# A two-layer diffusion trunk on one core: tap order, transposes on row halves, low parts of weights by accumulating transfers, and another layer-norm pacing

## The chip, the core and the metric

The kernel runs on one core of a Trainium2 chip. The metric is the device time of one execution in microseconds (us). The engines named below are PE (TensorE, matmuls; its weight loads are listed as PEld), DVE (VectorE), ACT (ScalarE), POOL (GpSimd) and SP (SyncE, which here only starts transfers).

## The reference

A trunk of two layers works on 256 latent tokens and 256 context tokens of width 1024. Each layer, cut to what matters here (the first six numbers of `mod`/`mod_c` are shifts, scales and gates made from the conditioning vectors):

```python
h  = modulate(rmsnorm(x,  norm1_g[l]), sh1, sc1)
hc = modulate(rmsnorm(xc, norm1_g[l]), csh1, csc1)
p  = h @ w_in[l]                       # GLU pair | q k v | branch gates
q, k = rope_2d(q), rope_2d(k)          # latent rows only
y_conv = conv_branch(p[..., :GLU_END], conv_dw[l], conv_dw_b[l], conv_ln_g[l], conv_ln_b[l], w_conv_out[l])
y_attn = merge_heads(neighbourhood_attention(q, k, v, k_c, v_c, na_rpb[l])) @ w_na_out[l]
x  = x + g1 * gated_merge(p[..., QKV_END:], y_conv, y_attn, w_out[l])
h2 = modulate(rmsnorm(x, norm2_g[l]), sh2, sc2)
x  = x + g2 * conv_ffn(h2, w_up[l], ffn_dw[l], ffn_dw_b[l], w_down[l])

def conv_branch(p_glu, dw, dw_b, ln_g, ln_b, w_o):
    a, g = jnp.split(p_glu, 2, axis=-1)
    u = dwconv1d(a * jax.nn.sigmoid(g), dw, dw_b)      # 31 taps, 512 channels
    return jax.nn.silu(layernorm(u, ln_g, ln_b)) @ w_o
```

Attention has 8 heads of 64; a latent query sees a window of the latent grid with a learned bias and all context keys under one softmax. In layer 0 the context tokens pass through the same weights and attend to each other; in layer 1 they give keys and values only. The output is the latent stream after a last RMS norm.

## The kernel before

Tokens stand in columns, channels in partitions. In layer 0 a matmul has 512 moving columns (256 latent and 256 context tokens), in layer 1 mostly 256.

**Weights.** They come in units of 128x1024 (512 KB). SP loads a unit into one of four buffers `raw` (L147 and L157 start loads), ACT rounds it to a high part `whi` (L160), DVE subtracts to get the low part `wlo` (L161); both have four buffers as well. `wunit` does this for one unit. Each product is three passes, `mm3` (L179 to L181): high weight by high activation, high weight by low activation, low weight by high activation. A group is one accumulation over a unit's eight blocks, 24 matmuls; in the two output branches of the token mixer it is twelve, and a unit has two groups. After a group, and in layer 0 also in its middle, `slot()` lets the side work run a step: taps, attention, the layer norm, modulation.

**Attention.** Class `Attention` takes head pairs as their queries and keys become ready. `products` computes scores of two heads on the 64-row halves of PE (L440). `scores` adds the bias and takes the maximum on DVE (L458), ACT exponentiates and sums, DVE inverts, ACT scales. `turn` transposes the probabilities, 128x128 at a time (L494 for latent queries, L499 for context), 16 transposes a turn, into the PSUM banks `sc`, `sc`, `pt` and `main`; ACT copies each bank to `pT`. `values` multiplies with V (L512) on 64-column tiles. `step` decides by a count of slots when the next turn, values and products are issued; in one step the turn of the scores before comes first, then the values of the turn before, then new products. There are six turns in layer 0 and four in layer 1.

**Convolution.** Each of four channel blocks has 31 taps on DVE (`conv_tap`, L591), issued two or three a slot; in layer 0 two `u` buffers hold the GLU outputs, so that taps of block j must be out before block j + 2 is written. The layer norm follows as side work: the four blocks are summed (two adds on POOL, L842 and L843, one on DVE), a matmul with ones (L847) gives the sum over channels, then squares, `rstd`, and the scaling.

**Modulation.** Part of the modulation numbers for later is made by `ada_dots`: DVE multiplies a 128x1024 weight tile with a broadcast row and sums (L271, two dots a tile), and part by `ada_half`, 32-column matmuls (L202) with transposes behind them (L228). The tiles come through the same four `raw` buffers. The number `pace[0]` says how many dot steps a slot makes.

**Behind attention** of layer 0 stand the remaining gates, the neighbourhood output branch (`U_NA`, with a gate multiply on DVE behind each group, L885) and the convolution output branch (`U_CO`, L890 to L893).

**Order.** The program is built once: the framework fixes the order of the instructions on each engine when it is built, by its own estimate of when each can run. `issue_after` adds an ordering to this. Each engine then executes its list in order and waits at the head of it.

Of the kernel before, what the change touches and what calls it, by code (L numbers as in the profile page):

```python
# [8 lines left out]
F32 = mybir.dt.float32  # L9
# [28 lines left out]
U_GLU0, U_V, U_IN, U_NA, U_CO, U_WO, U_UP, U_DN = 0, 2, 6, 36, 40, 44, 52, 96  # L38
NU = 118
T_GLU, T_Q, T_K, T_GATE = 0, 6, 10, 14  # L40

# [4 lines left out]
def trunk(ctx: ExitStack, tc: tile.TileContext, xt, cvec, crow, wall, wada, params, bias_t, rope_t, out):  # L46
# [136 lines left out]
    def group(ps, ws, xh, xl, c):  # L183
# [201 lines left out]
    class Attention:  # L385

        def __init__(self, l, eb, T, V, oh, ol):
            self.l, self.eb, self.T, self.V, self.oh, self.ol = l, eb, T, V, oh, ol  # L390
            self.todo, self.soft, self.pv, self.n, self.at = [], [], [], 0, 0
            self.ctx, self.pairs, self.last = [], 0, None

# [22 lines left out]
        def step(self, now=False):  # L416
            self.n += 1
            since = self.n - self.at
            if not now and (since < (4 if self.todo else 3 if self.soft else 2) or not self.todo and self.pairs < 4):
                return  # L420
            if self.todo and not now and self.n - self.todo[0][0] < 2:
                return
            self.at = self.n
            pv, self.pv = self.pv, []
            soft, self.soft = self.soft, []
            for what, its, pps in soft:
                with tc.issue_after(self.last.ins), tc.issue_after(self.done.ins):
# [3 lines left out]
            if self.todo:  # L431
                _, what, its = self.todo.pop(0)
                outs = [self.products(it, [psum(t) for t in tags]) for it, tags in zip(its, (("sc", "sc"), ("pt", "main")))]
                self.soft.append((what, its, [(self.scores if what == LAT else self.ctx_scores)(it, o) for it, o in zip(its, outs)]))

# [15 lines left out]
        def scores(self, it, out):  # L451
            qt, bt = it[1], it[-1]
            pps = []
            for i, ps in enumerate(out):

                mx = small([P, 1], "mx")
                p2, b2 = ps.rearrange("p (a k) -> p a k", a=2), bt[:, 2 * qt + i :: 4 - 2 * qt - i, :]
                dve.tensor_tensor_reduce(p2, p2, b2, -1.0, 3.0e38, ALU.add, ALU.min, mx)  # L458
                pp = self.eb.tile([P, 512], F32, tag="pp", bufs=4, name=nm("pp"))
                sm = small([P, 1], "sm")  # L460
                self.exp = act.activation(pp, ps, AF.Exp, bias=mx, scale=-1.0, accum_out=sm)
                ri = small([P, 1], "ri")
                dve.reciprocal(ri, sm)
                self.done = act.mul(pp, pp, ri)
                pps.append(pp)
            return pps

        def ctx_scores(self, it, out):
            pps = []
            for ps in out:  # L470
                mx = small([P, 2], "mx2")
                dve.tensor_reduce(mx, ps.rearrange("p (q k) -> p q k", q=2), AX.X, ALU.max, negate=True)
                pp = self.eb.tile([P, 512], F32, tag="pp", bufs=4, name=nm("pp"))
# [12 lines left out]
        def turn(self, what, its, pps):  # L486

            pts = [self.eb.tile([P, 4, S], F32, tag="pT", bufs=4, name=nm("pT")) for _ in range(2)]
            for n, tags in enumerate((("sc", "sc"), ("pt", "main"))):
                for i, pp in enumerate(pps[n]):  # L490
                    pt = psum(tags[i])
                    if what == LAT:
                        for kt in range(4):
                            pe.transpose(sl(pt, kt), sl(pp, kt), ident)  # L494
                        act.copy(pts[i][:, :, n * P : (n + 1) * P], pt.rearrange("p (k q) -> p k q", k=4))
                    else:
                        for t in range(2):
                            for kt in range(2):
                                pe.transpose(pt[:, kt * S + t * P : kt * S + (t + 1) * P], sl(pp, 2 * t + kt), ident)  # L499
                        act.copy(pts[i][:, 2 * n : 2 * n + 2, :], pt.rearrange("p (k q) -> p k q", k=2))  # L500
            js = [its[0][0]] if what == LAT else [it[0] for it in its]
            self.pv.append((what, js, pts))

        def values(self, what, js, pts, bank):
            po = psum(bank)
            kts = range(4) if what == LAT else range(2, 4)
            for n, j in enumerate(js):
                c = slice(n * S, (n + 1) * S)
                for kt in kts:
                    for i in range(2):  # L510
                        h = 2 * j + i
                        pe.matmul(  # L512
                            po[i * HD : (i + 1) * HD, c], self.V[kt][:, h * HD : (h + 1) * HD],
                            pts[i][:, 2 * n + kt - kts[0], :], start=kt == kts[0], stop=kt == kts[-1],
                        )
# [42 lines left out]
    for l in range(DEPTH):  # L558
# [5 lines left out]
        with ExitStack() if last else start as e1a:  # L564
# [17 lines left out]

            taps = []

            def conv_tap(j, t):
                w = par[:, l * NPAR + DW + j * TAPS + t : l * NPAR + DW + j * TAPS + t + 1]
                src = us[j % NU_][:, :, t : t + S]
# [4 lines left out]

            rate = [0]

            def conv_run():
                while True:
                    for _ in range(rate[0]):
                        if taps:
# [34 lines left out]
            with ExitStack() as e1b:  # L633
                eb = e1b.enter_context(tc.tile_pool(name=f"eb{l}", bufs=1))
                V = [eb.tile([P, CONV], F32, name=f"V{l}_{t}") for t in range(4)]
                att = Attention(l, eb, T, V, oh, ol)

# [107 lines left out]
                conv = conv_run()  # L745
                rate[0] = 3 if last else 2
                add_side(conv)
# [68 lines left out]
            with ExitStack() as e1c:  # L816
# [15 lines left out]
                def layer_norm():  # L832

                    while taps:
# [14 lines left out]
                    for j in range(KC):  # L849
                        dve.scalar_tensor_tensor(flat[j], pm[:, :T], -1.0 / CONV, flat[j], ALU.mult, ALU.add)  # L850
                        s2.add(flat[j], j == KC - 1)
                    yield
                    yield
                    pb = yield from rstd(s2, CONV, "po")
                    for j in range(KC):
# [7 lines left out]
                        yield  # L863
                    pace[0] = 0.4

# [359 lines left out]
```

## Time and profile before

| | us |
|---|---|
| three runs, median (lowest to highest) | 1127.05 (1126.9 to 1127.49) |
| the profiled execution | 1127.64 |
| its span, first to last instruction | 1125.9 |
| PE busy in it | 1114.1 |
| PE weight loads | 963.0 |
| DVE busy | 908.3 |
| ACT busy | 563.6 |
| POOL busy | 14.7 |

The mean granted TensorE clock is 0.998 of full speed. A row of a group reads: line, engine, operation, output and inputs, shape, count, then busy time in us and mean ns of one, then the idle time ahead of them and what ended it. A row of a timeline begins with its start and its length in us from the span's start. A matmul's length contains its way through the array; how fast they follow each other is read from start to start. Layer 0's attention lies between about 80 and 200 us, the stage behind it to 330 us.

### The profile page before, as it was taken

Reading aid. Unit: us, or ns where it says so; the run is one execution under the profiler, and the core shown is the slowest. Engines: PE = TensorE matmul, PEld = TensorE weight load, DVE = VectorE, ACT = ScalarE, POOL = GpSimd, SP = SyncE. Lnnn points to the kernel's source line nnn. Section 1 sums busy time; section 2 is a strip of 40 time slices with the busy share of each in tenths; the row PEclk is TensorE's granted clock in tenths of the full one; section 3 lists DMA queues with packets and bytes.
Section 4 is the critical chain, followed back from the end, with each engine's and each line's share of the span. In section 5 each row is a group of like instructions: output and inputs, shape, how many; then the busy total and the mean of one; then the engine's idle time right before and its main releaser. Section 6 shows DMA issues by size and latency. Waiting matters only on the chain.

```text
span 1125.9 us, 17731 instructions
## 1 busy us (share of the span) xinstructions
PE 1114.1 (99%) x6828; PEld 963.0 (86%) x6828; DVE 908.3 (81%) x1631; ACT 563.6 (50%) x934; POOL 14.7 (1%) x24
## 2 busy tenths in 40 slices
PE   9999999999999999999999999999999999999997
PEld 7778777787789988888888888989888999999997
DVE  5689999685778788888898555789996898988773
ACT  4347657542333543434343222544677667766642
POOL 0000000000000000000000000000000000000000
PEclk9999999999999999999999999999999999999999
DMA  9833231536734354554556665556433575565781
GB/s 364 282 94 103 75 118 38 206 97 214 245 118 138 114 161 150 168 169 149 168 171 215 219 191 186 180 181 187 145 126 121 167 250 163 188 194 181 219 268 58
DMA packets 53941, 190.83 MB, mean 169 GB/s; under 512 B 6240, under 2 KB 6496, under 8 KB 53856
## 3 DMA queue, kind: packets, MB, share of 16 engines
q1 hardware_dynamic: 53568, 189.65, 52.1%
q8 instruction: 54, 0.88, 0.3%
q14 instruction: 31, 0.25, 0.1%
q10 hardware_dynamic: 288, 0.04, 0.0%
HBM read 188.62 MB, written 1.05 MB: 168 GB/s over the span
## 4 chain that ended last, share of the span: by engine, by line
PE 83%; DVE 9%; issue 6%; ACT 2%; DMA 0%; POOL 0%; POOLq 0%; DVEq 0%; SPq 0%; ACTq 0%
PE main L179 24%; PE main L181 24%; PE main L180 24%; DVE cb L591 4%; PE main L644 4%; DVE wlo L161 1%; PE sc L181 1%; PE sc L179 1%; PE sc L180 1%; PE po L202 1%; PE po L512 1%; PE sc L129 1%; PE sc L440 0%; DMA sb<-in_crow 0%; PE sc L494 0%
## 5 line engine op out<-in xcount | busy, mean ns | idle before, releaser
L179 PE MATMUL main<-h,whi 128*128 128x256 f32 (+1 forms) x1328 | 446.7, 337 | 0.0
L181 PE MATMUL main<-h,wlo 128*128 128x256 f32 (+1 forms) x1328 | 442.9, 335 | 1.0 <-DVE wlo L161 1.0
L180 PE MATMUL main<-h,whi 128*128 128x256 f32 (+1 forms) x1328 | 442.2, 334 | 0.1
L160 ACT CAST whi<-raw 128x1024 fp32r<-128x1024 f32 (+1 forms) x244 | 252.3, 1039 | 285.5 <-PE main L180 131.5
L161 DVE TENSOR_TENSOR wlo<-raw,whi 128x1024 fp32r<-128x1024 f32 (+1 forms) x244 | 292.9, 1207 | 112.5 <-ACT whi L160 108.0
L179 PEld LDWEIGHTS main<-h,whi 128*128 128x128 f32 x1328 | 249.4, 188 | 32.1 <-issue 3.6
L181 PEld LDWEIGHTS main<-h,wlo 128*128 128x128 f32 x1328 | 249.3, 188 | 29.6 <-DVE wlo L161 1.5
L180 PEld LDWEIGHTS main<-h,whi 128*128 128x128 f32 x1328 | 249.8, 188 | 28.5 <-DVE h L367 0.5
L591 DVE SCALAR_TENSOR_TENSOR cb<-u,par,cb 128x512 f32<-128x512 f32 (+1 forms) x240 | 140.4, 609 | 1.4
L271 DVE CUSTOM_DVE_ANT_0 t<-raw,sb,par 128x1024 bf16<-128x1024 f32 x100 | 126.7, 1277 | 1.0 <-ACT sb L255 0.7
L179 PE MATMUL main<-fh,whi 128*128 128x256 f32 (+1 forms) x386 | 123.0, 319 | 0.0
L180 PE MATMUL main<-fl,whi 128*128 128x256 f32 (+1 forms) x386 | 122.9, 319 | 0.0
L181 PE MATMUL main<-fh,wlo 128*128 128x256 f32 (+1 forms) x386 | 122.9, 318 | 0.0
L180 PEld LDWEIGHTS main<-fl,whi 128*128 128x128 f32 x386 | 72.7, 188 | 5.6
L179 PEld LDWEIGHTS main<-fh,whi 128*128 128x128 f32 x386 | 72.7, 188 | 5.6
L181 PEld LDWEIGHTS main<-fh,wlo 128*128 128x128 f32 x386 | 72.7, 188 | 5.5
L963 ACT ACTIVATE t<-main,par 128x512 f32<-128x512 f32 (+1 forms) x82 | 50.6, 667 | 39.0 <-PE main L181 39.0
L964 DVE SCALAR_TENSOR_TENSOR t<-main,par,t 128x510 f32<-128x510 f32 (+1 forms) x82 | 47.5, 615 | 10.2 <-ACT t L963 9.8
L967 DVE SCALAR_TENSOR_TENSOR t<-main,par,t 128x510 f32<-128x510 f32 (+1 forms) x82 | 46.6, 609 | 0.0
L366 ACT ACTIVATE h<-t,mod 128x256 fp32r<-128x256 f32 x56 | 25.4, 502 | 36.1 <-DVE t L365 36.1
L898 DVE SCALAR_TENSOR_TENSOR x<-main,mod,x 128x256 f32<-128x256 f32 x48 | 22.1, 479 | 23.5 <-PE main L181 23.3
L644 PE MATMUL main<-whi,h 128*128 128x512 f32 x128 | 40.6, 402 | 0.1
(221 smaller groups left out, 1188.2 us busy)
## 6 DMA issues: line engine op xcount, KB each, us to landing
raw<-in_wall SPq DMA_DIRECT2D x239, 512.0 KB, 4.2
raw<-in_wada SPq DMA_DIRECT2D x88, 512.0 KB, 4.3
bias<-in_bias_t SPq DMA_DIRECT2D x8, 640.0 KB, 4.8
row<-in_wada SPq DMA_DIRECT2D x8, 512.0 KB, 4.7
sb<-in_crow SPq DMA_DIRECT2D x5, 512.0 KB, 6.0
x<-in_xt SPq DMA_DIRECT2D x8, 256.0 KB, 4.4
raw<-in_wall SPq DMA_DIRECT2D x8, 256.0 KB, 7.1
out<-t SPq DMA_DIRECT2D x3, 256.0 KB, 2.1
```

The costliest lines, as they stand in the source:

```text
L160: act.copy(hi[:, c], r[:, c])
L161: dve.tensor_tensor(lo[:, c], r[:, c], hi[:, c].bitcast(F32), ALU.subtract)
L179: pe.matmul(ps, w[0], xh, start=start, stop=False)
L180: pe.matmul(ps, w[0], xl, start=False, stop=False)
L181: pe.matmul(ps, w[1], xh, start=False, stop=stop)
L271: dve.tensor_tensor_reduce(tmp().bitcast(BF16), r, v, 1.0, pr(l, BADA + n, 1), ALU.mult, ALU.add, mods[l][:, n, s : s + 1])
L366: high = act.activation(hi[:, c], y[:, c], AF.Identity, bias=b)
L591: dve.scalar_tensor_tensor(cb[j], src, w, cb[j], ALU.mult, ALU.add)
L644: mm = pe.matmul(pv[t], h1[n == 1][k][:, c], w[n == 2][:, b], start=k + n == 0, stop=k == KD - 1 and n == 2)
L963: act.activation(c, pv_, AF.Identity, bias=pr(l, FDB + t, 1), scale=w[1])
L964: dve.scalar_tensor_tensor(c[:, :, 1:], pv_[:, :, : S - 1], w[0], c[:, :, 1:], ALU.mult, ALU.add)
L967: dve.scalar_tensor_tensor(c[:, :, : S - 1], pv_[:, :, 1:], w[2], c[:, :, : S - 1], ALU.mult, ALU.add)
```

## The change

1. **Turning on row halves.** `turn` issues each 128x128 transpose as two, for rows 0 to 63 and 64 to 127, with 64 columns of the identity moving, into two banks; a turn is 32 transposes. `pT` is one tile for two heads, the copies write it in another layout.
2. **Low parts by transfers.** For 26 units (`ADDED`: 19 in layer 0, 7 in layer 1, all among GLU, query, key and gate units) the new `wadded` lets ACT write the high part and its negative, and POOL starts an accumulating transfer that adds `raw`. The memory for POOL's transfer descriptors is set to 1024.
3. **Taps.** Each tap is ordered behind the score maximum issued last. Layer 0 has four `u` buffers instead of two, and three taps a slot instead of two. In `step`, layer 0 can issue a turn without new products; the products then come in the next step (`late`).
4. **Layer norm of layer 0.** All three block sums are on DVE; four slots pass instead of two before `rstd`; `pace[0]` is 0.2 during the norm and 1.0 behind it (1.0 and 0.4 before). Layer 1 keeps its values.

```diff
+ADDED = {*((0, U_IN + i) for i in range(19)), *((1, U_IN + i) for i in (7, 8, 9, 14, 15, 16, 17))}
...
+    def wadded(l, u):
+
+        r = raw_unit(wall[l, u])
+        hi = wp.tile([P, UW], F32R, tag="whi", bufs=4, name=nm("whi"))
+        lo = wp.tile([P, UW], F32R, tag="wlo", bufs=4, name=nm("wlo"))
+        act.copy(hi, r)
+        act.mul(lo, hi.bitcast(F32), -1.0)
+        pool.dma_start(lo, r, accum_op=ALU.add)
+        return hi, lo
+
     def unit8(l, u, at=None):
-        w = wunit(l, u, at)
+        w = wadded(l, u) if (l, u) in ADDED else wunit(l, u, at)
...
-            if not now and (since < (4 if self.todo else 3 if self.soft else 2) or not self.todo and self.pairs < 4):
+            alone = not self.l and self.soft and not self.pv and not self.late
+            if not now and since < (4 if self.todo or alone else 3 if self.soft else 2) and not self.late:
                 return
-            if self.todo and not now and self.n - self.todo[0][0] < 2:
+            if not now and not alone and not self.todo and self.pairs < 4:
                 return
+            if not now and not alone and self.todo and self.n - self.todo[0][0] < 2:
+                return
+            if self.late:
+                self.late, self.at = False, self.n
+                return self.issue()
+            if alone and not now:
+                self.late = True
...
-                dve.tensor_tensor_reduce(p2, p2, b2, -1.0, 3.0e38, ALU.add, ALU.min, mx)
+                self.after[0] = dve.tensor_tensor_reduce(p2, p2, b2, -1.0, 3.0e38, ALU.add, ALU.min, mx)
...
+                outs = [psum(t).rearrange("p (i s q) -> p i s q", i=2, s=4) for t in tags]
                 for i, pp in enumerate(pps[n]):
...
+                    for s in range(4):
+                        src = s if what == LAT else s % 2 * 2 + s // 2
+                        for pt, r in zip(outs, HALF):
+                            pe.transpose(pt[:, i, s], sl(pp, src)[r], ident[r, r])
+                for pt, r in zip(outs, HALF):
...
-                        for kt in range(4):
-                            pe.transpose(sl(pt, kt), sl(pp, kt), ident)
...
-            NU_ = KC if last else 2
+            NU_ = KC
...
             def conv_tap(j, t):
+                if after[0] is not None:
+                    with tc.issue_after(after[0].ins):
+                        tap(j, t)
+                else:
+                    tap(j, t)
...
-                rate[0] = 3 if last else 2
+                rate[0] = 3 if last else 3.0
...
-                    pace[0] = 1.0
+                    pace[0] = 1.0 if last else 0.2
...
-                    pool.tensor_tensor(sm[:, :T], flat[0], flat[1], ALU.add)
-                    pool.tensor_tensor(sm[:, :T], sm[:, :T], flat[2], ALU.add)
+                    eng = pool if last else dve
+                    eng.tensor_tensor(sm[:, :T], flat[0], flat[1], ALU.add)
+                    eng.tensor_tensor(sm[:, :T], sm[:, :T], flat[2], ALU.add)
...
-                    yield
-                    yield
+                    for _ in range(2 if last else 4):
+                        yield
...
-                    pace[0] = 0.4
+                    pace[0] = 0.4 if last else 1.0
...
-    nc = bacc.Bacc("TRN2", target_bir_lowering=False, num_devices=1)
+    nc = bacc.Bacc("TRN2", target_bir_lowering=False, num_devices=1, dynamic_dma_scratch_size=1024)
```

Lines of the changed kernel in the rows below: L180 to L182 are the three passes, L162 the low part on DVE, L199 and L200 ACT's two passes of an added unit, L213 the 32-column matmuls, L282 the dots, L463 the products, L518 the transposes, L921 the gate multiply.

PE, layer 0, around the first turn, before: a unit group, the turn, the products of the next pair.

```order
L181 MATMUL main_972<-h_189,wlo_975 128x512
L494 MATMUL sc_1009<-ident,pp_845 128x128 x4
L494 MATMUL sc_1015<-ident,pp_853 128x128 x4
L494 MATMUL pt_1021<-ident,pp_861 128x128 x4
L494 MATMUL main_1027<-ident,pp_869 128x128 x4
L440 MATMUL sc_1033<-qk_967,qk_921 128x512
L440 MATMUL sc_1034<-qk_967,qk_921 128x512
```

The same place of the change; rows that repeat a pair are left out.

```order
L182 MATMUL main_945<-h_189,wlo_949 128x512
L518 MATMUL sc_984<-ident,pp_861 128x64
L518 MATMUL sc_985<-ident,pp_861 128x64
...
L518 MATMUL pt_1004<-ident,pp_877 128x64
L518 MATMUL main_1005<-ident,pp_877 128x64
...
L180 MATMUL main_1035<-h_182,whi_1038 128x512
```

The transposes come in pairs into two banks, and the unit group's next matmuls, not the products, follow this turn.

DVE, layer 0, around the second unit of the neighbourhood branch, before (`g` a gate, `t_` and `mod` a dot and its sum):

```order
L885 TENSOR_TENSOR g_9_2284<-main_2603,g_9_2284 128x512
L161 TENSOR_TENSOR wlo_2679<-raw_2677,whi_2678 128x1024
L885 TENSOR_TENSOR g_10_2332<-main_2628,g_10_2332 128x512
L271 ISA t_2703,mod_108<-raw_2701,sb_2022,par 128x1024
L271 ISA mod_108 128x1
L271 ISA t_2705,mod_108<-raw_2701,sb_2025,par 128x1024
```

The low part 2679 stands here ahead of the second unit's gate multiplies and is used by the third unit. In the change the same place reads:

```order
L921 TENSOR_TENSOR g_9_2405<-main_2710,g_9_2405 128x512
L162 TENSOR_TENSOR wlo_2737<-raw_2735,whi_2736 128x1024
L282 ISA t_2756,mod_108<-raw_2754,sb_2160,par 128x1024
L282 ISA mod_108 128x1
L282 ISA t_2758,mod_108<-raw_2754,sb_2163,par 128x1024
```

The low part behind the multiply of `main_2710` is now that of the second unit itself. On PE the change reads there:

```order
L182 MATMUL main_2710<-oh_3_205,wlo_2671 128x512
L180 MATMUL main_2741<-oh_0_202,whi_2736 128x512
L181 MATMUL main_2741<-ol_0_206,whi_2736 128x512
L180 MATMUL main_2761<-oh_0_202,whi_2736 128x512
L181 MATMUL main_2761<-ol_0_206,whi_2736 128x512
L213 MATMUL sc_2768<-raw_2769,sil 32x256 x4
L182 MATMUL main_2741<-oh_0_202,wlo_2737 128x512
```

Both groups of the unit begin with their high parts, half a visit to the 32-column tiles stands between, and then comes the first matmul that needs the low part 2737. Before, the twelve matmuls of a group stood together and the visit in one piece.

More of the change, by code (lines that the diff above doesn't have):

```diff
@@ L385, in trunk, with __init__ @@
     class Attention:
-        def __init__(self, l, eb, T, V, oh, ol):
+        def __init__(self, l, eb, T, V, oh, ol, after):
+            self.after = after
             self.l, self.eb, self.T, self.V, self.oh, self.ol = l, eb, T, V, oh, ol
             self.todo, self.soft, self.pv, self.n, self.at = [], [], [], 0, 0
-            self.ctx, self.pairs, self.last = [], 0, None
+            self.ctx, self.pairs, self.last, self.late = [], 0, None, False
         def pair(self, j, q, k, bt, last):
@@ L430, in step, with issue @@
                 self.values(*work, "sc" if work[0] == CTX and not (soft or self.todo) else "po")
[L431 to L434, printed above, removed]
+            if self.todo and not self.late:
+                self.issue()
+        def issue(self):
+            _, what, its = self.todo.pop(0)
+            outs = [self.products(it, [psum(t) for t in tags]) for it, tags in zip(its, (("sc", "sc"), ("pt", "main")))]
+            self.soft.append((what, its, [(self.scores if what == LAT else self.ctx_scores)(it, o) for it, o in zip(its, outs)]))
         def product(self, out, q, k, c, d):
```

30 lines of the change are left out of this document (16 added, 14 removed).

## The prediction

> **What bounds the kernel now.** I read the page first, then the windows of the attention stretch and of the stage behind it, then the timeline at one turning, and last the groups kept apart by shape.
>
> ```profile
> span 1125.9 us, 17731 instructions
> PE 1114.1 (99%) x6828; PEld 963.0 (86%) x6828; DVE 908.3 (81%) x1631; ACT 563.6 (50%) x934; POOL 14.7 (1%) x24
> L181 PE MATMUL main<-h,wlo 128*128 128x256 f32 (+1 forms) x1328 | 442.9, 335 | 1.0 <-DVE wlo L161 1.0
> 100.00:120.00 20.00, 20.00 (x131) 16.15 (x130) 20.00 (x39) 16.72 (x34) 0.00 (x0) 1.00 0.44 138
> 160.00:180.00 20.00, 20.00 (x124) 15.61 (x124) 20.00 (x39) 15.56 (x29) 0.00 (x0) 1.00 0.28 79
> 260.00:280.00 20.00, 20.00 (x111) 14.95 (x110) 10.40 (x17) 4.61 (x7) 0.00 (x0) 1.00 0.59 194
> ```
>
> The page's first part gives PE 1114.1 of 1125.9 us, at a granted clock of 1.00 in these windows. A window reads: its bounds, its length, then the busy time of PE, PEld, DVE, ACT and POOL with their counts, the clock, the DMA share and GB/s. In the two windows of layer 0's attention DVE is as full as PE, 20.00 of 20. Yet the low-part matmuls of the whole program (L181) wait 1.0 us in sum for DVE's low parts. So DVE is full there with work that has no early deadline, the taps, and PE sets the pace. Taking load from DVE moves nothing by itself; the time changes only where PE's own instructions get shorter or more numerous, or where a new wait reaches PE. Behind attention DVE is half empty (10.40 of 20 in the last row).
>
> The profiled execution took 1127.64 us, its span and 1.7 us around it; the median of the three runs is 0.6 lower. I sum against 1127.64 and take off 0.6 at the end.
>
> **Turning on row halves.** Before, a turn is 16 transposes of 128 rows; ten turns make 160. Now each transpose is a pair, rows 0 to 63 and 64 to 127, each with 64 moving columns, into two banks.
>
> ```profile
> 100.45 0.39 PE L181 MATMUL main<-h,wlo 128*128 128x512 f32 x1
> 100.68 1.04 PE L494 MATMUL sc<-ident,pp 128*128 128x128 f32 x8
> 101.55 0.60 PE L494 MATMUL pt<-ident,pp 128*128 128x128 f32 x4
> 101.99 0.60 PE L494 MATMUL main<-ident,pp 128*128 128x128 f32 x4
> 102.52 1.16 PE L440 MATMUL sc<-qk,qk 64*128 64x512 f32 x6
> ```
>
> Eight transposes from 100.68 to 101.55 are 0.109 us each; 160 of them 17.4 us. A 512-column matmul takes the 0.23 us from 100.45 to 100.68, 0.45 ns a column, a transpose 0.85 ns a column. Either it is bound by its moving columns, at twice the price, and then a pair of 64-column halves, side by side on two row groups, takes 0.055; or it is bound by loading 128 stationary columns, which the halves do not shorten. The rows nearest to the question:
>
> ```profile
> L494 PEld LDWEIGHTS sc<-ident,pp 128*128 128x128 f32 x64 | 7.4, 141 | 0.8
> L512 PEld LDWEIGHTS po<-pT,V 128*64 128x64 f32 x144 | 9.5, 136 | 5.4 <-issue 1.3
> L202 PEld LDWEIGHTS po<-raw,sil 128*32 128x32 f32 x128 | 3.2, 109 | 4.0 <-issue 2.2 <-ACT whi L680 0.4
> L180 PEld LDWEIGHTS main<-h,whi 128*128 128x128 f32 x1328 | 249.8, 188 | 28.5 <-DVE h L367 0.5 <-issue 0.2 <-DVE h L893 0.2
> L336 PE MATMUL pt<-one,ss 128*128 128x1 f32 x32 | 4.1, 237 | 0.1
> 717.60 0.61 PE L336 MATMUL pt<-one,ss 128*128 128x1 f32 x4
> 114.75 0.28 PE L440 MATMUL main<-qk,qk 64*128 64x256 f32 x1
> 114.87 0.28 PE L440 MATMUL main<-qk,qk 64*128 64x256 f32 x1
> ```
>
> A load's record grows with its columns: 109 ns for 32, 136 for 64, 188 for 128, about 0.82 ns a column. The transposes' own load is recorded at 141 ns, as if it had some 70 columns: 47 ns or 57 ns less than an ordinary load of the same tile, so it should not hold 0.109. Against that, four matmuls with one moving column (717.60) take 0.61 us, of which 0.24 is the last one's tail: 0.12 apiece, and only a load can cost that. Pairs of product halves with 256 columns come every 0.12 us (114.75, 114.87), two loads included, so loads on two row groups do overlap: a pair of transposes costs at most 0.12. Ends for a pair: 0.055 and 0.12. I take 0.06, since the transposes' own row (141) is nearer to the question than the one-column matmuls: 160 x (0.109 - 0.06) = 7.8 us gained. At 0.12 it would be 1.8 us lost.
>
> The Trainium skill speaks against this edit: TensorE: Matmul & The Clock Gate, section "LDWEIGHTS (loading the stationary operand)", says that a load takes its columns divided by 1.2, in ns, however few rows it has, an estimate of 107 ns for 128 columns. By that rule a pair would gain nothing; the trend of the three load rows agrees, the 141 does not. That is the second rival.
>
> Halves have the tile shape of the products (64 rows) and no longer that of the unit groups. What a change of shape costs:
>
> ```profile
> 266.05 0.40 PE L181 MATMUL main<-oh,wlo 128*128 128x512 f32 x1
> 266.38 1.07 PE L202 MATMUL sc<-raw,sil 128*32 128x256 f32 x16
> 267.38 0.50 PE L179 MATMUL main<-oh,whi 128*128 128x512 f32 x1
> 267.72 0.39 PE L180 MATMUL main<-ol,whi 128*128 128x512 f32 x1
> ```
>
> Into the small tiles 0.33 us pass instead of 0.23, and the first full tile after them has 0.34: about 0.1 at either end, and up to 0.2 where the loads too have to restart. By PE's order the change adds some seven changes of shape in layer 0 and three in layer 1. At 0.16 each (between 0.1 and 0.2) 1.6 us. Turning: -7.8 + 1.6 = -6.2 us; ends -8.7 + 1.0 = -7.7 and +1.8 + 2.0 = +3.8.
>
> **Low parts by adding transfers.** 26 units lose DVE's subtraction; ACT writes the negated high part instead, and POOL starts a transfer of 512 KB that adds `raw`.
>
> ```profile
> L161 DVE TENSOR_TENSOR wlo<-raw,whi 128x1024 fp32r<-128x1024 f32 x238 | 288.8, 1220 | 112.2 <-ACT whi L160 108.0 <-PE sc L181 3.2 <-PE sc L440 0.3
> L160 ACT CAST whi<-raw 128x1024 fp32r<-128x1024 f32 x238 | 248.8, 1050 | 285.5 <-PE main L180 131.5 <-DMA raw<-in_wall 128.7 <-issue 11.8
> raw<-in_wall SPq DMA_DIRECT2D x239, 512.0 KB, 4.2
> 872.80 1.05 ACT L160 CAST whi<-raw 128x1024 fp32r<-128x1024 f32 x1 [1.49 <-PE main L180]
> 875.64 1.05 ACT L160 CAST whi<-raw 128x1024 fp32r<-128x1024 f32 x1 [1.51 <-PE main L180]
> ```
>
> DVE loses 26 x 1.22 = 31.7 us and ACT gains 26 x 1.05 = 27.3, hidden on an engine that waits 285.5 us ahead of its casts; neither is on PE's path. The transfer's time t has no row: it reads two tiles on the chip and writes one, and the nearest row is a load of the same size, 4.2 us. What hides it is the lead of four buffers. Layer 0: 24 matmuls x 0.23 = 5.6 us a unit, four units 22.3; less load 4.2 and two passes of ACT 2.1, 16 us are left for t. Layer 1: casts in steady flow come every 2.84 us (872.80, 875.64), four units 11.4, less 6.3: 5.1 us are left. So t up to 5.1 costs nothing; each us beyond it costs the seven units of layer 1 a quarter of a us each, 1.75 us in all, until 16 us, where layer 0 joins. I take t = 4.2 and nothing. No gain is possible here beyond the 1.0 us that L181 waits. Behind a late transfer on POOL's queue stand the next transfers only, but for two row-sum adds of layer 1 whose inputs come from taps.
>
> The Trainium skill has two rules on such a transfer, and no run here shows either. DMA: Bandwidth & Descriptors, "Anatomy of one DMA — SWDGE (gpsimd) path", gives about 2.0 us and its bytes at 436 GB/s, an estimate of 3.2 us, which stays hidden. SBUF — State Buffer, "SBUF: two separate sides", says that DVE operations holding the port pair shared with POOL keep POOL from writing descriptors; beside a DVE that is busy 20.00 of 20 us that could make t long, the third rival.
>
> **Taps and adds.** Tying taps behind score maxima lets the maxima go first; the taps lag into DVE time that the 31.7 us set free. PE does not wait for score maxima now, so nothing is gained; the cost, if the cover were gone, is that the layer norm's inputs come late, and its first matmul now stands 60 group matmuls, 14 us, earlier on PE. The two POOL adds become DVE adds of under 0.7 us each, under main groups: nothing. The row-sum matmul itself stays, so "fewer row sums" is fewer POOL adds.
>
> **What the earlier norm pushes together.** Behind the norm the fourteen dot tiles of the adaptive modulation (two dots each) follow at full pace instead of 0.4, and now stand among the last gates and the neighbourhood and convolution output groups.
>
> ```profile
> L271 DVE CUSTOM_DVE_ANT_0 t<-raw,sb,par 128x1024 bf16<-128x1024 f32 x100 | 126.7, 1277 | 1.0 <-ACT sb L255 0.7 <-DMA raw<-in_wada 0.4
> 263.28 1.28 DVE L271 CUSTOM_DVE_ANT_0 t<-raw,sb,par 128x1024 bf16<-128x1024 f32 x1
> 264.48 1.28 DVE L271 CUSTOM_DVE_ANT_0 t<-raw,sb,par 128x1024 bf16<-128x1024 f32 x1
> 280.45 1.21 DVE L161 TENSOR_TENSOR wlo<-raw,whi 128x1024 fp32r<-128x1024 f32 x1
> 281.58 0.15 DVE L238 TENSOR_TENSOR mod<-mod,par 128x4 f32<-128x4 f32 x1
> 281.75 0.69 DVE L885 TENSOR_TENSOR g<-main,g 128x512 f32<-128x512 f32 x1
> 282.36 0.15 DVE L295 SCALAR_TENSOR_TENSOR gain<-mod,par 128x2 f32<-128x2 f32 x1
> ```
>
> Start to start a dot takes 1.20 us, a low part 1.13, a gate multiply 0.61. From the low part of the second output unit to that of the fifth, DVE's order holds six dot tiles (6 x 2.40 = 14.4), six multiplies (3.7), three low parts (3.4) and a us of small ones: 22.5 us. PE needs 3 x 5.58 = 16.7 for those units, three visits to the small tiles at 1.2 each (266.05 to 267.72 less two matmuls) and 0.7 for visits that are now split in two: 21.0. So DVE, half empty before, is the bound there by 1.5 us. On top, the low part of each next unit stands behind the gate multiply of the group just finished: 0.61 + 1.22 us after PE's last matmul, under which PE has four high-part matmuls (0.93) and half a visit (0.6): 0.3 short, and 1.4 with a dot just begun. Four such units: at most 5.6 us. Ends 0 and 5.6; I take 2.5, a us over the sum. The split visits: two more entries and exits, 0.7 us.
>
> **Sum.** -6.2 + 0 + 2.5 + 0.7 = -3.0: 1127.6 - 3.0 = 1124.6 profiled, less 0.6: **1124.0 us**.
>
> **The rivals.** *No stall behind the norm*: the adds and dots finish in time, as the half-empty DVE of 260 to 280 suggests; -6.2 + 0.7, 1121.5. *The halves are bound by their loads* (the one-column matmuls speak for it, the 141 ns against): +1.8 + 1.6 + 3.2 = +6.6, 1133.6, slower; it decides from a pair of 0.08 us on, where what turning still gains is eaten by the 3.2. *Late transfers* in layer 1: at t = 9, 3.9 x 1.75 = 6.8 on top of the forecast, 1130.8, slower; it decides once t exceeds 6.8, where it has eaten the forecast's 3.0. For it: adding on the way is more than a load; against: 16 us of cover in layer 0. *Gains given back*: the full 5.6 behind the norm, -6.2 + 5.6 + 0.7 = +0.1, 1127.1: the change then does not do what it says, DVE's relief having only moved its load.
>
> **How the numbers follow.** Forecast 0.26, no stall 0.20, load-bound halves 0.22, late transfers 0.16, given back 0.16. About 0.2%, 2.25 us, is what a measurement of this kernel can tell from no change. Faster: 0.20 and 0.24 of the forecast, 0.44. Slower: 0.22 + 0.16 = 0.38. Within: 0.18. The low end is turning at its best, L181's wait gone and no stall: 1127.6 - 7.7 - 1.0 - 0.6, 1118; the high end load-bound halves with the full stall: 1133.6 + 3.1, 1137. The faster cases alone lie between 1118 and 1125.
>
> **What would show it.** After: a turn of 32 halves lasting about 1.0 us instead of 1.74 shows the gain; 1.9 shows load-bound halves. POOL's transfers should land within 5 us of issue; waits of L182 for low parts made by L201 show the third rival. Between 255 and 300 us PE should show gaps of 0.3 to 1.4 us ending on low parts behind gate multiplies. I am wrong in the mechanism if PE waits for score maxima, or if the tapped norm comes late.

## The result, and the profile after

The changed kernel takes 1132.56 us (median of five runs, 1130.94 to 1133.27) against 1127.05 (five runs, 1126.9 to 1127.49): ratio 1.0045, interval 1.003 to 1.006. It is slower by 0.45%, where 0.3% faster was forecast. The profiled execution is the fastest of the five, 1130.94 us, 3.3 us above that of before. Its page:

```profile
span 1129.2 us, 18139 instructions
PE 1111.4 (98%) x6988; PEld 956.2 (85%) x6988; DVE 887.7 (79%) x1607; ACT 589.3 (52%) x960; POOL 36.3 (3%) x50
wlo<-raw POOLq DMA_DIRECT2D x26, 512.0 KB, 5.3
```

PE has less to do (1111.4 against 1114.1 us) in a longer span, so PE has new waits. The windows, in the columns of before:

```profile
100.00:120.00 20.00, 18.80 (x135) 14.06 (x134) 14.83 (x32) 17.19 (x33) 1.74 (x2) 1.00 0.68 172
160.00:180.00 20.00, 20.00 (x170) 15.07 (x170) 17.78 (x35) 16.93 (x32) 0.89 (x1) 1.00 0.49 127
260.00:280.00 20.00, 18.11 (x99) 12.35 (x97) 12.09 (x22) 3.45 (x5) 0.00 (x0) 1.00 0.58 209
280.00:300.00 20.00, 16.57 (x91) 11.20 (x92) 15.75 (x32) 2.47 (x3) 0.00 (x0) 1.00 0.75 256
```

In attention (100 to 120) DVE fell from 20.00 to 14.83, and PE lost 1.2 us, most of it one wait of 0.98 us for copies of `pT`. The large loss is behind the norm: PE is busy 34.7 of 40 us between 260 and 300, where before it was busy throughout. PE's timeline there, only rows with a wait:

```profile
270.99 0.64 PE L213 MATMUL sc<-raw,sil 128*32 128x256 f32 x8 [0.57 <-DMA raw<-in_wada]
272.63 0.50 PE L182 MATMUL main<-oh,wlo 128*128 128x512 f32 x1 [1.00 <-DVE wlo L162]
278.68 0.50 PE L180 MATMUL main<-oh,whi 128*128 128x512 f32 x1 [0.18 <-ACT whi L161]
280.56 0.50 PE L182 MATMUL main<-oh,wlo 128*128 128x512 f32 x1 [0.70 <-DVE wlo L162]
287.73 0.64 PE L213 MATMUL sc<-raw,sil 128*32 128x256 f32 x8 [0.62 <-DMA raw<-in_wada]
288.86 0.44 PE L239 MATMUL pt<-ident,t 128*128 128x128 f32 x2 [0.49 <-ACT t L232]
295.47 0.50 PE L180 MATMUL main<-sh,whi 128*128 128x512 f32 x1 [1.58 <-ACT whi L161]
297.41 0.64 PE L213 MATMUL sc<-raw,sil 128*32 128x256 f32 x8 [0.18 <-DMA raw<-in_wada]
```

In sum these are 5.3 us. Two waits are low parts behind a gate multiply, as reckoned (1.00 and 0.70). Five, 3.1 us, go back to loads: three for tiles of the 32-column matmuls, two for casts that had waited for their unit's load. The last, 0.49, is for ACT's copy of a 32-column product. The last cast, its load's issue on SP and the issues ahead of it:

```profile
280.53 7.61 SPq L148 DMA_DIRECT2D raw<-in_wada  x4
288.43 0.33 SPq L158 DMA_DIRECT2D raw<-in_wall  x1
294.37 1.04 ACT L161 CAST whi<-raw 128x1024 fp32r<-128x1024 f32 x1 [5.57 <-DMA raw<-in_wall]
```

SP starts loads in order and needs a free buffer for each. Four loads of dot tiles and small-tile matrices stand ahead of the unit's load from 280.53 on; it is issued at 288.43, the cast can begin at 294.37, PE at 295.47. The four `raw` buffers are shared by weights, dots and 32-column matmuls, and the crowded dots hold them: of 15.8 us that SP waits between 279 and 297 us, 9.0 are for a dot to be done with its buffer.

In the runs below the kernel before takes 1127.73 to 1127.79 us; each ratio is against the kernel before measured beside it. That is some 0.7 us above the 1127.05 of the result.

### The profile page after: what moved, and what is told of

It is laid out like the page before. It is cut to its first block, busy times and chain, and to the rows that moved or that the text cites. A ratio compares the mean times of both kernels' runs of the same rounds, so it can differ in the third digit from the quotient of the medians.

```text
span 1129.2 us, 18139 instructions
## 1 busy us (share of the span) xinstructions
PE 1111.4 (98%) x6988; PEld 956.2 (85%) x6988; DVE 887.7 (79%) x1607; ACT 589.3 (52%) x960; POOL 36.3 (3%) x50
## 4 chain that ended last, share of the span: by engine, by line
PE 90%; DVE 5%; ACT 2%; DMA 2%; issue 1%; POOL 0%; SPq 0%; DVEq 0%; ACTq 0%; POOLq 0%
PE main L180 26%; PE main L182 26%; PE main L181 25%; PE main L679 4%; DVE cb L623 2%; DMA raw<-in_wada 2%; PE po L536 1%; PE sc L180 1%; PE sc L182 1%; PE sc L181 1%; PE po L213 1%; PE sc L463 1%; PE sc L130 1%; ACT whi L161 1%; PE pt L463 0%
## 5 line engine op out<-in xcount | busy, mean ns | idle before, releaser
L180 PE MATMUL main<-h,whi 128*128 128x256 f32 (+1 forms) x1328 | 447.3, 338 | 0.0
L182 PE MATMUL main<-h,wlo 128*128 128x256 f32 (+1 forms) x1328 | 443.4, 335 | 1.0 <-DVE wlo L162 1.0
L161 ACT CAST whi<-raw 128x1024 fp32r<-128x1024 f32 (+1 forms) x218 | 225.5, 1038 | 253.4 <-DMA raw<-in_wall 123.9
L162 DVE TENSOR_TENSOR wlo<-raw,whi 128x1024 fp32r<-128x1024 f32 (+1 forms) x218 | 262.2, 1208 | 91.8 <-ACT whi L161 88.2
L180 PEld LDWEIGHTS main<-h,whi 128*128 128x128 f32 x1328 | 249.8, 188 | 32.0 <-issue 3.9
L182 PEld LDWEIGHTS main<-h,wlo 128*128 128x128 f32 x1328 | 249.7, 189 | 29.4 <-DVE wlo L162 1.4
L623 DVE SCALAR_TENSOR_TENSOR cb<-u,par,cb 128x512 f32<-128x512 f32 (+1 forms) x240 | 144.0, 612 | 3.2
L282 DVE CUSTOM_DVE_ANT_0 t<-raw,sb,par 128x1024 bf16<-128x1024 f32 x100 | 126.3, 1278 | 3.8 <-DMA raw<-in_wada 3.8
L180 PE MATMUL main<-fh,whi 128*128 128x256 f32 (+1 forms) x386 | 123.1, 319 | 0.0
L182 PE MATMUL main<-fh,wlo 128*128 128x256 f32 (+1 forms) x386 | 123.0, 319 | 0.0
L180 PEld LDWEIGHTS main<-fh,whi 128*128 128x128 f32 x386 | 72.8, 189 | 5.6
L182 PEld LDWEIGHTS main<-fh,wlo 128*128 128x128 f32 x386 | 72.8, 189 | 5.5
L1025 ACT CAST fh<-t 128x256 fp32r<-128x256 f32 (+1 forms) x43 | 22.0, 511 | 36.2 <-DVE t L1015 35.7
```

What stands on the lines that cost most here:

```text
L161: act.copy(hi[:, c], r[:, c])
L162: dve.tensor_tensor(lo[:, c], r[:, c], hi[:, c].bitcast(F32), ALU.subtract)
L180: pe.matmul(ps, w[0], xh, start=start, stop=False)
L182: pe.matmul(ps, w[1], xh, start=False, stop=stop)
L282: dve.tensor_tensor_reduce(tmp().bitcast(BF16), r, v, 1.0, pr(l, BADA + n, 1), ALU.mult, ALU.add, mods[l][:, n, s : s + 1])
L623: dve.scalar_tensor_tensor(cb[j], src, w, cb[j], ALU.mult, ALU.add)
```

## The experiments

**e1: the two pace numbers put back.**

```diff
-                    pace[0] = 1.0 if last else 0.2
+                    pace[0] = 1.0
...
-                    pace[0] = 0.4 if last else 1.0
+                    pace[0] = 0.4
```

> The change with its two pace numbers of layer 0 put back (1.0 during the norm, 0.4 behind it); all else of the change stays. Theory crowding: the dots issued at full pace behind the norm fill the four raw buffers and delay casts and low parts, and the gaps of PE between 260 and 300 us (11.4 us of excess against 4.1 before) go: about 7 us less than the change's 1132.6, near 1125.3, and those runs scatter by under 1 us again. Rival transfers: the time comes from the adding transfers elsewhere, the pace is innocent: 1131 to 1133, and PE still has gaps there. Rival turning: products waiting for the copies of pT (1.25 and 0.98 us) are the cost: 1131 to 1133 too, but without gaps between 260 and 300.

Measured 1125.51 us, ratio 0.9982 (0.9973 to 0.9991): 7.0 us less than the change by the medians, 5.8 by the two profiled executions (1130.94 and 1125.11), and 0.2% faster than before. The stage behind the norm in its windows:

```profile
260.00:280.00 20.00, 20.00 (x112) 15.00 (x111) 8.62 (x16) 3.46 (x5) 0.00 (x0) 1.00 0.54 184
280.00:300.00 20.00, 20.00 (x112) 15.02 (x111) 12.99 (x24) 6.48 (x9) 0.00 (x0) 1.00 0.69 227
```

PE is full again, with a DVE of 8.62 and 12.99 where the change had 12.09 and 15.75. That the pace makes these gaps is shown; the scatter did not narrow as expected (one of eleven runs took 1128.7).

**f4 and g1: one of the two numbers put back.** f4 keeps 0.2 during the norm and takes 0.4 behind it; g1 takes 1.0 during the norm and keeps 1.0 behind it.

> The change with one number put back: pace 0.4 behind the norm instead of 1.0; 0.2 during the norm stays. Theory: the full pace behind the norm is the whole of the 7 us: 1125 to 1126.5, and no gaps between 260 and 300 us but the 4.1 us of visits. Rival: the slow pace during the norm holds dots back until then and is part of it: 1128 or more.

> The change with the other pace number put back: 1.0 during the norm, as before; 1.0 behind it stays. With 0.2 during and 0.4 behind the program took 1140.7, waiting at the next norm for dots that were not done. Theory: the slow pace during the norm is the cause; it stacks the dots up behind the norm, where either they crowd (1.0 behind) or come too late (0.4 behind): with 1.0 in both places 1125 to 1126.5 and little more than 4 us of excess on PE between 260 and 300 us. Rival: full pace behind the norm crowds the buffers by itself: 1130 or more.

f4 took 1140.67 us, ratio 1.0111 (1.0096 to 1.0126): the theory fails, and the rival (1128 or more) has the direction but not the size. g1 took 1126.47, ratio 0.9989 (0.9980 to 0.9998), at the upper edge of its theory. In f4 the stage of 260 to 300 us is clean, and PE waits at the second RMS norm instead (rows of PE's timeline with a wait, the last dot on DVE, and one window):

```profile
360.37 0.43 PE L362 MATMUL po<-ident,rs 128*128 128x128 f32 x2 [2.00 <-POOL rs L357]
362.89 0.79 PE L180 MATMUL sc<-h,whi 128*128 128x256 f32 x2 [2.10 <-ACT h L377]
366.93 0.58 PE L180 MATMUL main<-h,whi 128*128 128x256 f32 x1 [2.39 <-ACT whi L161]
373.20 0.58 PE L182 MATMUL sc<-h,wlo 128*128 128x256 f32 x1 [5.48 <-DVE wlo L162]
358.18 1.28 DVE L282 CUSTOM_DVE_ANT_0 t<-raw,sb,par 128x1024 bf16<-128x1024 f32 x1
365.00:370.00 5.00, 0.80 (x2) 0.50 (x2) 3.01 (x8) 3.19 (x7) 0.00 (x0) 0.50 0.27 108
```

The dots run to 359.4 on DVE, 16 of them between 320 and 360 us against 6 before. Behind them in DVE's list stand the norm's sums and the gains made from the dots, so the norm's scaled activations, and behind those the buffers, casts and low parts, are late: four waits of 12 us in sum. The clock column of the last row is a second cost: 0.50. So no single number is the cause in the way that I had put it. The slow pace during the norm holds back dots; then full pace crowds them into the output branches (7 us against e1), and slow pace brings them too late for the next norm (15 us). Between 260 and 300 us DVE starts 14 dots in the change, 6 in the kernel before, 4 in e1 and f4, and 8 in g1, where PE is idle for 0.5 us. At 1.0 during the norm, 1.0 behind it costs about 1 us, and the intervals of g1 and e1 overlap.

**e2: layer norm and pace as before the change.** Beside e1's edit the two sums go back to POOL and two slots stand ahead of `rstd`.

```diff
-                    eng = pool if last else dve
-                    eng.tensor_tensor(sm[:, :T], flat[0], flat[1], ALU.add)
-                    eng.tensor_tensor(sm[:, :T], sm[:, :T], flat[2], ALU.add)
+                    pool.tensor_tensor(sm[:, :T], flat[0], flat[1], ALU.add)
+                    pool.tensor_tensor(sm[:, :T], sm[:, :T], flat[2], ALU.add)
...
-                    for _ in range(2 if last else 4):
-                        yield
+                    yield
+                    yield
```

> As the run before, and the two sums back on POOL and two slots instead of four ahead of rstd: layer norm and pace as before the change. Theory crowding: the adds and slots cost nothing by themselves, within 1 us of the run with the pace alone put back (1124.5 to 1126.5). Rival: the earlier norm is worth something by itself, then this is over 1 us slower than that run.

1128.94 us, ratio 1.0014 (1.0005 to 1.0022), 3.4 us over e1: the rival holds, adds and slots are worth something. PE reaches the norm's matmuls before DVE has their sums (1.59 us for `ss`) and stops; soon after it has started again the clock falls:

```profile
218.00:220.00 2.00, 2.00 (x10) 1.35 (x8) 2.00 (x4) 0.13 (x1) 0.00 (x0) 1.00 0.79 197
220.00:222.00 2.00, 0.41 (x4) 0.33 (x4) 2.00 (x4) 0.00 (x0) 0.00 (x0) 1.00 0.27 72
222.00:224.00 2.00, 2.00 (x12) 1.73 (x12) 2.00 (x4) 0.00 (x0) 1.00 (x1) 0.80 0.78 240
224.00:226.00 2.00, 2.00 (x6) 1.60 (x5) 0.12 (x2) 1.05 (x1) 1.01 (x1) 0.50 0.46 107
```

The early arrival points to the two slots, but which of the two edits does it was not separated.

**e3: before, with the turning on row halves alone.** `turn` and `values` as in the change, nothing else.

> Before, with only the turning on row halves. From the change's trace a pair takes 0.073 us on average with its ends, 11.6 us for all against 18.4: 6.8 us less, and about 1 us back for changes of tile shape: 1121 (1120 to 1122.5). Rival waits: with a shorter turn the products behind it wait for ACT's copies out of the banks, about 1 us at several of the ten turns, and the gain shrinks to under 3 us: 1124 to 1127. Rival loads (a pair costs 0.12): 1130.

1129.17 us, ratio 1.0014 (1.0005 to 1.0023): 1.4 us slower, no gain at all. The number lies near the rival of loads (1130), but the transposes did get shorter, as the table below shows; it is the rival of waits that comes, larger than expected. What PE waits for in this run (us in sum, times, longest), four of its rows:

```profile
PE pt L228 <- ACT t L221: 1.5, 1, 1.5
PE sc L440 <- ACT pT L498: 1.3, 3, 0.8
PE pt L495 <- ACT pp L482: 1.1, 1, 1.1
PE po L513 <- DVE ol L520: 0.7, 1, 0.7
```

Only the first of these stood in before, with 0.6. They are the work behind the softmax: copies of `pT` out of the banks that the next products need, scaled probabilities, `ol`. I took the starts of all PE instructions in the two attention stretches (60 to 215 and 780 to 880 us) and added up the time from each start to the next by kind; a wait counts for the instruction ahead of it:

```
us                 before   e3   change   e1    f1    f2    f3    g3
transposes           18.6  14.6   11.6   11.6  18.4  13.1  20.0  12.1
values               18.8  19.8   19.8   19.8  19.1  20.0  21.1  19.8
products             16.6  17.9   18.2   18.2  16.6  18.7  16.8  17.1
changes of shape       62    70     76     72    62    75    66    72
```

The last row counts changes of tile shape in the whole program. The halves take 7 us off the transposes where nothing waits; values and products give 2.6 back in the change, 2.3 in e3, where the transposes too keep 3 us of waits. By these rows e3 would still gain 1.7 us, and it loses 1.4. Of the other 3.1 us the longer wait at L228 is 0.9, and eight more changes of shape stand in it too; the rest was not followed.

**e4 and g4: before, with adding transfers alone**, all 26, and only the 19 of layer 0 (`wadded`, `ADDED` and the descriptor memory as in the change).

> Before, with only the 26 low parts by adding transfers (and the descriptor memory of 1024). They land 5.3 us after their issue in the change's trace, against 5.1 us of cover reckoned in layer 1. Theory hidden: 1127.0 within 1 us, DVE's 31.7 us buy nothing and PE has no new gap. Rival late transfers: waits of PE's low-part matmuls for them in layer 1, 1129 or more. Rival relief: DVE was a bound somewhere, under 1125.

> The kernel before, with adding transfers in layer 0 only. With all 26 it took 8.3 us more; its trace shows 4.0 us of waiting for a transfer of layer 1 at 818, PE at half clock for 6 us behind it, and 1.8 us at 191 in layer 0. Theory: without layer 1's units 6.5 us of that go and 1.8 stay: 1129.5 (1128 to 1130.5). Rival: the transfers of layer 0 cost by themselves (loads delayed by them): 1133 or more.

e4 took 1136.06 us, ratio 1.0074 (1.0061 to 1.0086); g4 1129.26, ratio 1.0017 (1.0008 to 1.0026). The late transfers are shown for layer 1, which takes 6.8 of the 8.3 us that e4 loses. What g4 loses is no late transfer: PE's waits there have none for a transfer, but a new one of 1.6 us of transposes for ACT's scaled probabilities. In e4, ACT, POOL and PE there, and one window:

```profile
815.87 0.42 ACT L779 ACTIVATE qk<-t 128x256 fp32r<-128x256 f32 x1 [0.88 <-DVE t L776]
816.46 1.05 ACT L200 ACTIVATE wlo<-whi 128x1024 fp32r<-128x1024 f32 x1
817.91 0.86 POOL L201 DMA_DIRECT2D wlo<-raw  x1 [4.52 <-ACT wlo L200]
822.80 0.58 PE L182 MATMUL main<-h,wlo 128*128 128x256 f32 x1 [3.80 <-DMA wlo<-raw]
824.00:826.00 2.00, 2.00 (x12) 2.00 (x11) 0.00 (x0) 0.00 (x0) 0.57 (x1) 0.50 0.86 246
```

The transfer itself takes 4.9 us, from 817.91 to 822.80, within the cover that I had reckoned. Late is its start: ACT's negation stands behind four copies of `pT` and activations of which one waits for DVE's rotary chain, which stands among taps. So at this stop it is not t but what is queued ahead of ACT's second pass that uses up the cover. Elsewhere t itself is long: the seven transfers of layer 1 land 4.8 to 10.3 us after their issue in e4, 7.8 in the median. PE stops for 4 us and then runs at clock 0.50 for 6.

**f1, f2 and f3: e1 without halves, without adding transfers, without both.**

> The run with the pace put back (1125.5), and in it the turning whole again, 128 rows at a time. Theory: halves save 6.7 us of transposes there (11.65 against 18.4 in sum) and lose 3.0 to waits behind the turns (0.35, 1.25, 0.38, 0.99): without them 1129.2 (1128 to 1130.5). Rival, from halves alone on the kernel before (1129.2 against 1127.7): what they save comes back as waits in any surroundings: 1124 to 1126.

> The run with the pace put back, and in it the 26 low parts again subtracted on DVE. Theory relief: the ordered taps and the earlier norm need the 31.7 us of DVE, without them taps and norm come late and PE waits: 1128 or more. Rival hidden: DVE still is no bound, and the two waits for low parts (0.63, 1.24) go: 1123.5 to 1125.5.

> The run with the pace put back, without halves and without adding transfers: what is left of the change are the ordered taps, the split steps and the adds and slots of the norm. If the parts add up, it lies as far from the run without halves as the run without adding transfers from the one with both. Theory needs-each-other: taps and norm alone are worth nothing or cost, 1127 to 1131. Rival: they are what makes the change fast, under 1126.

| run | us | ratio to before (interval) |
|---|---|---|
| e1, all but the pace | 1125.51 | 0.9982 (0.9973 to 0.9991) |
| f1, without halves | 1128.30 | 1.0005 (0.9996 to 1.0013) |
| f2, without adding transfers | 1128.89 | 1.0009 (1.0000 to 1.0018) |
| f3, without both | 1131.41 | 1.0034 (1.0021 to 1.0046) |

So with ordered taps and the earlier norm the halves are worth 2.8 us and the adding transfers 3.4, and they add up: without both 5.9 us are lost. Taps, split steps and norm by themselves cost 3.6 us, just above the theory's range. In f3 the transposes take 20.0 and the values 21.1 us by the table above, together 3.7 more than before: values and transposes stand mixed on PE there, since probabilities come late, and one bank of transposes waits 1.3 us:

```profile
116.17 0.66 PE L517 MATMUL main<-ident,pp 128*128 128x128 f32 x4 [1.29 <-ACT pp L487]
```

That this is the whole of the 3.6 us was not tested, and the ordered taps, the extra `u` buffers and the split steps were never run apart.

**g2: a sigmoid behind the copies of `pT`.** In e1 the products of the second step wait from 112.6 to 113.6 us. PE and ACT of e1:

```profile
110.67 1.95 PE L536 MATMUL po<-pT,V 128*64 128x256 f32 x16
113.60 1.46 PE L463 MATMUL sc<-qk,qk 64*128 64x256 f32 x12 [0.98 <-ACT pT L521]
111.18 1.28 ACT L641 ACT_TABLE_LOAD   x1
112.47 0.60 ACT L641 ACTIVATE t<-main 128x512 f32<-128x512 f32 x1
112.97 1.07 ACT L521 COPY pT<-sc 128x512 f32<-128x512 f32 x2
```

A load of ACT's function table (1.28 us) and a GLU sigmoid stand ahead of the copies that free the products' banks.

```diff
+                with tc.issue_after(copied[0].ins) if copied[0] is not None and not last else ExitStack():
+                    act.activation(sg[:, :T], pg[:, :T], AF.Sigmoid)
```

The third block's `glu` is also called one slot later, behind the turn, and `copied[0]` is the last copy.

> The run with the pace put back (1125.5), with the sigmoid of the third GLU block ordered behind ACT's copies of pT: its table load (1.28 us) and itself (0.6) stood ahead of the copies for which PE's products waited 1.25 us at 112. A negation of 1.05 us takes their place, so the copies come 0.8 us earlier. Theory: 0.8 us less, 1124.7, and a gap of 0.4 to 0.5 left there. Rival: the products wait for something else, and nothing changes: 1125.5 and a gap of 1.25.

1125.30 us, ratio 0.9984 (0.9974 to 0.9994). The wait shrank as expected, from 0.98 to 0.15, and the products start at 112.80 instead of 113.60:

```profile
112.80 1.46 PE L464 MATMUL sc<-qk,qk 64*128 64x256 f32 x12 [0.15 <-ACT pT L522]
```

What waited is shown; the 0.2 us by which the medians differ is not told apart from none.

**g3: e1 with adding transfers in layer 0 only.**

```diff
-ADDED = {*((0, U_IN + i) for i in range(19)), *((1, U_IN + i) for i in (7, 8, 9, 14, 15, 16, 17))}
+ADDED = {(0, U_IN + i) for i in range(19)}
```

> The run with the pace put back, with adding transfers in layer 0 only (19 units); the seven of layer 1 are subtracted on DVE again. Theory: layer 1 has too little cover (landing took 6.0 us in the median, 9.0 at most, against 5.1 reckoned): its waits at 786 (1.24, for a transfer) and 810 (0.99, copies behind a negation on ACT) go: 1123.3 to 1124.5. Rival: layer 1 needs the relief of DVE as well: 1126 or more.

1123.48 us, ratio 0.9962 (0.9948 to 0.9975): the fastest of all, 4.3 us below before and 2.0 below e1. e1's wait for a transfer, in the view of PE's waits, is gone in g3, and its waits for copies of `pT` fall from 1.8 to 1.2 us in sum. In e1 the transfer's wait read:

```profile
PE main L182 <- DMA wlo<-raw: 1.1, 1, 1.1
```

That wait of e1 ends at 787.68, on a transfer that POOL had started at 780.22: some 7.5 us, and here it is the transfer itself that is longer than the 5.1 us of cover. By the medians the 19 units of layer 0 bring some 5.4 us in this program (f2 less g3), and the seven of layer 1 cost 2.0.

## Why the prediction was wrong

**The crowding behind the norm** was the step that failed: right in place, wrong in size, and in mechanism only half right. I had put it at 2.5 us, at most 5.6, with 0.7 for split visits, 3.2 in all; putting the pace back takes 7.0 away (5.8 by the profiled executions). One half came: the two low parts that waited (1.00 and 0.70) fit the reckoned 0.3 to 1.4. (With a dot just begun, 0.3 + 1.20 is 1.5 and not 1.4, so "at most" should have been 6.0.) The other half did not: DVE was not the bound by 1.5 us. It is busy 27.8 of the 40 us (12.09 and 15.75) and itself waits for tiles. What I left out is the ring of `raw` buffers: I counted DVE's time and PE's, and not that each dot tile holds a buffer and a place in SP's order until DVE is done with it. The waits that go back to loads (0.57, 0.62, 0.18, and 1.58 and 0.18 through casts) are 3.1 us against 1.7 for low parts, and the chain of work that ended last between 255 and 300 us lies to 40.8% in loads of modulation tiles. The cause was put in one number where it takes both: the slow pace during the norm holds the dots back, and full pace behind it crowds them; with either number put back PE stays busy there but for 0.5 us (f4, g1).

This step is the largest miss, 3.8 us by the medians, but by itself it would have brought the forecast of 3.0 us faster only to about 0.8 slower. The other terms follow. The nearness of 1132.56 to the 1133.6 of the load-bound rival is chance, since that rival's mechanism did not come.

**Turning.** The pair was sized right. In e1, 16 halves into `sc` start at 109.17 and those into the next banks at 109.72:

```profile
109.17 0.71 PE L518 MATMUL sc<-ident,pp 64*128 64x64 f32 x16
109.72 0.22 PE L518 MATMUL pt<-ident,pp 64*128 64x64 f32 x1
```

0.55 us for eight pairs, 0.069 each where I took 0.06; load-bound halves at 0.12 are refuted. With its ends a turn takes 1.16 us on average (11.6 for ten), where about 1.0 was forecast. The ten changes of shape came too (72 against 62); what one of them costs was not measured apart. What failed is that I let a shorter turn cost nothing behind it: 6.2 us were forecast, 2.8 came in the change's surroundings (f1 less e1) and none on the kernel before (e3), because copies and scaled probabilities that the long turns had covered, in one place behind a table load, are now waited for.

**Low parts by transfers.** t, taken as 4.2, is 5.3 in the median of all 26 in the change; in layer 1, where the cover was reckoned at 5.1, it is 6.1 there and 6.8 in e1. I forecast nothing either way; they bring 3.4 us in e1's surroundings and cost 8.3 alone. Layer 1 was rightly named as the short one: its seven units cost 2.0 us in e1 (g3), where the reckoned 1.75 us for each us beyond 5.1 would give 3.0 at 6.8. In e1 the transfer itself was late; in e4 the cover was used up by ACT's second pass in its queue, which I had not reckoned. In the change's own profile PE has no wait of 0.5 us or more for a transfer. And "taking load from DVE moves nothing by itself" held on the kernel before (g4 is no faster) and failed in the change's surroundings. The waits of f2 that e1 lacks or has smaller, in the view of PE's waits:

```profile
PE main L182 <- DVE wlo L162: 2.1, 3, 1.0
PE pt L239 <- ACT t L232: 1.3, 1, 1.3
PE pt L518 <- ACT pp L487: 0.6, 1, 0.6
PE sc L463 <- ACT qk L803: 0.5, 1, 0.5
```

Low parts and ACT's probabilities and activations come later there. That they do so because DVE, with its subtractions back, serves the softmax and the rotary chain later is argued, not tested.

**Taps and adds** were put at nothing. Without halves and transfers they cost 3.6 us (f3), where I had seen no cost because PE did not wait for score maxima: it waits for scaled probabilities instead (1.29 us in f3). The adds and slots of the norm save 3.4 with the pace put back (e2 against e1).

Step by step, from before to f3, e1 and the change, the runs give 3.6 for taps and norm, -5.9 for halves and transfers together and 7.0 for the pace, 4.8 in sum. The result has 5.5, since the kernel before measured 0.7 less beside it.

## What to carry to other kernels

A pace that spreads side work must be judged with the buffers that the work holds: work put off comes back where its inputs share a ring with the main stream's, or at the point that needs its result. Shortening a stage on the bounding engine pays only as far as the next stage's inputs are ready; list what the long stage had covered (copies out of its banks, table loads, scalings) and time them ahead of the edit. Moving work from a full engine to a transfer puts a new wait into another engine's order; look at what stands ahead of the instruction that starts it, and time the transfer in the stage with the least cover.

## What the runs showed of the hardware

A stop of PE can cost more than its length: after 4.0 us (e4) the granted clock was 0.50 for some 6 us, and after 1.75 us (e2, around 220) and 1.80 us (g4, around 192) it fell to 0.50 for about 3, some 1.5 to 2 us after PE had started again; after 1.25 us (e1) it stayed at 1.00. The Trainium skill, TensorE: Matmul & The Clock Gate, section "What's actually happening", has the clock fall after an idle window of about 3.4 us; the 4.0 us of e4 agree with that, the 1.75 us of e2 and 1.80 us of g4 are shorter than it. In the change's profile a stop of 1.75 us at 293.5 left the clock at 1.00, so near this length it goes either way. That the change's times scatter over 2.3 us for this reason is not shown: its slowest run has a clock of 0.996 and the fastest 0.998, but the second slowest (1132.98 us) has 0.998 too.

An accumulating transfer of 512 KB within the chip's own memory took 4.4 to 8.0 us from issue to landing in the change, 5.3 in the median, and POOL was busy 0.87 us with each.
